# Average pooling 2x2: summing each tile in two halves one behind the other

## Chip, cores, metric

One core of one Trainium2 chip. The metric is device time in microseconds (us); a profiled execution has a span, from the first to the last instruction, about 2 us shorter than its reported time (kernel before: 3100.3 of 3102.09 us).

## Reference

```python
x: float32 (32, 128, 256, 256), kernel_size 2, stride 2
output[:, :, i, j] = np.mean(x[:, :, 2*i:2*i+2, 2*j:2*j+2], axis=(2, 3))    # (32, 128, 128, 128)
```

1073.74 MB are read and 268.44 MB written, with three adds and one multiplication per output.

## The kernel before

A unit is a pair of input rows on each of 128 partitions. A tile has 32 units (8.39 MB in, 2.10 MB out). There are 127 whole tiles and one that is cut into pieces of 16, 8 and 8 units. Two input buffers; SP issues loads, DVE sums, ACT scales and issues stores.

```python
    def sums(it, dst, pieces=1):                       # DVE
        dve.tensor_add(out=it[:, :, 0:w], in0=it[:, :, 0:w], in1=it[:, :, w:]).then_inc(halfway)   # row sum
        take(dve, halfway)
        for g in halves(pieces):                       # column sums
            dve.tensor_add(out=dst[:, g], in0=it[:, g, 0:w:2], in1=it[:, g, 1:w:2]).then_inc(summed)

    def tile_sums(b):
        take(dve, stored[b], 16)
        take(dve, loaded[b], 16)
        sums(ins[b], res[b], 2)

    def tile_scale(b, done, frees=True):               # ACT
        for k, g in enumerate(halves()):
            take(act, summed)
            if k and frees:
                act.sem_inc(free[b])                   # both halves summed: the input buffer is free
            scale(res[b][:, g], done)
    # ... scale_store: tile_scale, wait for both scalings, issue the store
    # ... SP: two loads, then for each further tile take(sp, free[b]); load
```

## Time and profile before

| what | value | how to read it |
|---|---|---|
| time | 3102.11 us | median of three, 0.11 us between lowest and highest |
| DVE, ACT busy | 54%, 16% | neither is near full |
| DMA | 433 GB/s | flat in the steady stretch |
| DVE per tile | 13.33 us from first start to last end, then 10.84 idle | idle until the next load has landed |

The lines behind the last three rows are in the prediction. The starts of the first four tiles, from DVE's timeline (columns: start, duration, engine, line, operation, shapes; in brackets the idle time before and what ended it):

```profile
23.07 8.69 DVE L95 TENSOR_TENSOR in_tile<-in_tile 128x8192 f32<-128x8192 f32 x1 [23.07 <-DVEq L68]
...
42.41 8.69 DVE L95 TENSOR_TENSOR in_tile<-in_tile 128x8192 f32<-128x8192 f32 x1 [6.00 <-DVEq L68]
...
67.11 8.69 DVE L95 TENSOR_TENSOR in_tile<-in_tile 128x8192 f32<-128x8192 f32 x1 [11.37 <-DVEq L68]
...
91.31 8.69 DVE L95 TENSOR_TENSOR in_tile<-in_tile 128x8192 f32<-128x8192 f32 x1 [10.87 <-DVEq L68]
```

Tile starts are landings of loads, since DVE waits for each. It also waits for the store of two tiles earlier (`stored[b]`). From the third on the tile starts are 24.2 us apart. The last store of the kernel:

```profile
3094.17 0.34 ACTq L169 DMA_DIRECT2D out_dram<-res  x1
```

### The profile page before, as it was taken

The numbers are of one execution on the slowest core, as the hardware profiler recorded it, in microseconds if no ns is written. First come the engines' busy times: TensorE is split into PE (matmuls) and PEld (weight loads), VectorE is DVE, ScalarE is ACT, GpSimd is POOL, SyncE is SP. The second block draws the span as 40 slices with busy tenths as digits, with TensorE's granted clock in tenths as the row PEclk, the third lists the DMA queues.
The fourth block names the chain that finished last, engine by engine and source line by source line (L and its number), as shares of the span: only waits on it lengthen the run. The fifth ranks groups of instructions, "written<-read, shape, count | busy, mean of one in ns | idle before, by whom it ended". The sixth has DMA issues, their size and how long they took to land. (4 is left out here: it accounts for less than half of the span.)

```text
span 3100.3 us, 2993 instructions
## 1 busy us (share of the span) xinstructions
DVE 1688.1 (54%) x387; ACT 490.3 (16%) x258; POOL 0.2 (0%) x4
## 2 busy tenths in 40 slices
DVE  4555555555555555555555555555555555555556
ACT  1111111111111111111111111111111111111111
POOL 0000000000000000000000000000000000000000
DMA  9999999999999999999999999999999999999999
GB/s 418 438 438 424 440 431 431 440 426 436 440 426 437 440 423 439 438 424 440 428 435 440 426 436 440 426 437 440 423 440 438 424 440 427 435 440 426 436 440 413
DMA packets 37440, 1342.19 MB, mean 433 GB/s; under 512 B 4160, under 2 KB 4160, under 8 KB 4416
## 3 DMA queue, kind: packets, MB, share of 16 engines
q1 hardware_dynamic: 19008, 1077.94, 80.3%
q10 hardware_dynamic: 18432, 264.25, 19.9%
HBM read 1073.74 MB, written 268.44 MB: 433 GB/s over the span
## 5 line engine op out<-in xcount | busy, mean ns | idle before, releaser
L95 DVE TENSOR_TENSOR in_tile<-in_tile 128x8192 f32<-128x8192 f32 (+1 forms) x130 | 1112.9, 8561 | 1385.7 <-DVEq L68 1385.7
L106 ACT ACTIVATE res<-res 128x2048 f32<-128x2048 f32 (+1 forms) x257 | 489.0, 1903 | 2569.5 <-ACTq L68 2569.5
L98 DVE TENSOR_TENSOR res<-in_tile 128x2048 f32<-128x2048 f32 (+1 forms) x257 | 575.4, 2280 | 19.0
L106 ACT ACT_TABLE_LOAD x1 | 1.3, 1283 | 34.3 <-ACTq L68 34.3
L250 POOL MEMSET const-bfloat16-1.0<- 128x1 bf16 x1 | 0.1, 101 | 0.0
L250 POOL MEMSET const-uint8-127<- 128x1 uint8 x1 | 0.1, 101 | 0.0
L250 POOL MEMSET const-float32-0.0<- 128x1 f32 x1 | 0.1, 98 | 0.2 <-issue 0.2
L250 POOL MEMSET const-float32-1.0<- 128x1 f32 x1 | 0.1, 98 | 0.0
## 6 DMA issues: line engine op xcount, KB each, us to landing
out_dram<-res ACTq DMA_DIRECT2D x125, 2048.0 KB, 32.5
in_tile<-in_x_dram SPq DMA_DIRECT2D x1, 4096.0 KB, 19.9
in_tile<-in_x_dram SPq DMA_DIRECT2D x2, 2048.0 KB, 26.6
out_dram<-res SPq DMA_DIRECT2D x2, 2048.0 KB, 23.7
in_tile<-in_x_dram SPq DMA_DIRECT2D x127, 34.3
out_dram<-res ACTq DMA_DIRECT2D x1, 1024.0 KB, 9.0
out_dram<-res ACTq DMA_DIRECT2D x2, 512.0 KB, 6.3
```

The lines of the kernel that those rows point to most:

```text
L95: dve.tensor_add(out=it[:, :, 0:w], in0=it[:, :, 0:w], in1=it[:, :, w:]).then_inc(halfway)
L98: dve.tensor_add(out=dst[:, g], in0=it[:, g, 0:w:2], in1=it[:, g, 1:w:2]).then_inc(summed)
L106: act.mul(out=dst, in_=dst, mul=0.25).then_inc(done)
L250: nc = _bacc.Bacc("TRN2", target_bir_lowering=False, num_devices=1)
```

## The change

Intent: the first half can be scaled while the second is still summed, because its column sum no longer waits for the row sum of the whole tile.

```diff
-    def sums(it, dst, pieces=1):
+    def sums(it, dst):
         dve.tensor_add(out=it[:, :, 0:w], in0=it[:, :, 0:w], in1=it[:, :, w:]).then_inc(halfway)
         take(dve, halfway)
-        for g in halves(pieces):
-            dve.tensor_add(out=dst[:, g], in0=it[:, g, 0:w:2], in1=it[:, g, 1:w:2]).then_inc(summed)
+        dve.tensor_add(out=dst, in0=it[:, :, 0:w:2], in1=it[:, :, 1:w:2]).then_inc(summed)
 
     def tile_sums(b):
         take(dve, stored[b], 16)
         take(dve, loaded[b], 16)
-        sums(ins[b], res[b], 2)
+        for g in halves:
+            sums(ins[b][:, g], res[b][:, g])
```

(`halves` becomes a plain list of the same two slices.)

More of the change, by code (lines that the diff above doesn't have):

```diff
@@ L82, in _pool_2x2 @@
         a = b
-    def halves(pieces=2):
-        if pieces == 1:
-            return [slice(None)]
-        return [slice(0, TILE // 2), slice(TILE // 2, TILE)]
+    halves = [slice(0, TILE // 2), slice(TILE // 2, TILE)]
     def load(t, b):
         sp.dma_start(out=ins[b], in_=xt[t]).then_inc(loaded[b], 16)
-    def sums(it, dst, pieces=1):
+    def sums(it, dst):
         dve.tensor_add(out=it[:, :, 0:w], in0=it[:, :, 0:w], in1=it[:, :, w:]).then_inc(halfway)
         take(dve, halfway)
-        for g in halves(pieces):
-            dve.tensor_add(out=dst[:, g], in0=it[:, g, 0:w:2], in1=it[:, g, 1:w:2]).then_inc(summed)
+        dve.tensor_add(out=dst, in0=it[:, :, 0:w:2], in1=it[:, :, 1:w:2]).then_inc(summed)
     def tile_sums(b):
@@ L108, in tile_scale @@
     def tile_scale(b, done, frees=True):
-        for k, g in enumerate(halves()):
+        for k, g in enumerate(halves):
             take(act, summed)
```

## The prediction

> **What bounds the kernel now.** I read the page first, then the DMA view of a long steady stretch, then the timeline of one tile and of the end, because a share over the whole run cannot say which wait ends last.
>
> ```profile
> span 3100.3 us, 2993 instructions
> DVE 1688.1 (54%) x387; ACT 490.3 (16%) x258; POOL 0.2 (0%) x4
> DMA  9999999999999999999999999999999999999999
> HBM read 1073.74 MB, written 268.44 MB: 433 GB/s over the span
> ```
>
> No compute engine is near full: DVE, which does all the adds, works 54% of the time. The sixteen DMA engines are busy in every slice. The bytes are fixed by the task: 1342.19 MB at 433 GB/s are 3100 us, the whole span. In a steady stretch of 20 tiles (1400 to 1884 us) the DMA view gives the same 433 in each of its 40 slices, with no dip, so transfers never wait for compute there. One tile is 8.39 MB in and 2.10 MB out; 10.49 MB at 433 GB/s are 24.2 us, and tiles do follow each other at 24.2 us in the timeline (1493.88, 1518.05, 1542.25).
>
> The timeline of one tile:
>
> ```profile
> 1493.88 8.69 DVE L95 TENSOR_TENSOR in_tile<-in_tile 128x8192 f32<-128x8192 f32 x1 [10.87 <-DVEq L68]
> 1502.71 4.50 DVE L98 TENSOR_TENSOR res<-in_tile 128x2048 f32<-128x2048 f32 x2
> 1505.13 1.91 ACT L106 ACTIVATE res<-res 128x2048 f32<-128x2048 f32 x1 [20.02 <-ACTq L68]
> 1507.40 1.91 ACT L106 ACTIVATE res<-res 128x2048 f32<-128x2048 f32 x1 [0.36 <-ACTq L68]
> 1507.56 0.33 SPq L92 DMA_DIRECT2D in_tile<-in_x_dram  x1
> 1509.54 0.34 ACTq L118 DMA_DIRECT2D out_dram<-res  x1
> 1518.05 8.69 DVE L95 TENSOR_TENSOR in_tile<-in_tile 128x8192 f32<-128x8192 f32 x1 [10.84 <-DVEq L68]
> ```
>
> DVE takes 1507.21 - 1493.88 = 13.33 us per tile and then idles 10.84 us until the next load has landed. The load into the buffer just emptied is issued at 1507.56. At that moment the load of the other buffer is still under way, until about 1518.0. So the load queue is refilled 10.5 us before it would run dry. That slack is the number to hold the change against.
>
> At the end the picture is different:
>
> ```profile
> 3065.64 8.69 DVE L95 TENSOR_TENSOR in_tile<-in_tile 128x8192 f32<-128x8192 f32 x1 [10.84 <-DVEq L68]
> 3074.48 4.49 DVE L98 TENSOR_TENSOR res<-in_tile 128x2048 f32<-128x2048 f32 x2
> 3078.89 4.42 DVE L95 TENSOR_TENSOR in_tile<-in_tile 128x4096 f32<-128x4096 f32 x1
> 3083.45 2.29 DVE L98 TENSOR_TENSOR res<-in_tile 128x2048 f32<-128x2048 f32 x1
> 3085.66 2.29 DVE L95 TENSOR_TENSOR in_tile<-in_tile 128x2048 f32<-128x2048 f32 x1
> ...
> 3091.67 1.23 DVE L98 TENSOR_TENSOR res<-in_tile 128x1024 f32<-128x1024 f32 x1
> ```
>
> From the landing of the last whole tile (3065.64) DVE works with no idle time to 3092.90: the three pieces of the remaining tile are there before DVE comes to them (no idle time is listed in front of them). Then come the last scaling (3093.02) and the last store (issued at 3094.17, landed 5.2 us later). So in the last 35 us DVE is on the path, once. But the DMA engines are full there as well: by the view of stretches they still move 381 to 463 GB/s in every 2 us from 3086 to 3098, and stop only after that.
>
> [...]
>
> [...]
>
> [...] the second load ran beside DVE's first adds, from 23.07 to 42.41 us, at 434 GB/s; the first, with DVE idle, at 427, its start-up included. So another order of DVE's reads and writes should not change the transfer rate.
>
> **The change part by part.** For 127 whole tiles DVE's order becomes row sum A, column sum A, row sum B, column sum B, where it was one row sum of both halves and then two column sums. The listing of both instruction streams shows nothing moved on ACT, SP or POOL, only the same instructions at other line numbers. The remaining tile's three pieces are as before.
>
> 1. DVE, removed: 127 row sums of 8192 elements at 8.692 us = 1103.9 us. Added: 254 of 4096 elements at 4.418 us = 1122.2 us. DVE's busy time rises by 18.3 us, from 1688 to about 1706 us (55%). Column sums stay 2.288 us.
> 2. Waits on DVE: a column sum starts 0.14 us after its row sum ends (1502.57 to 1502.71), since it waits for it; with two such pairs there is one more wait of 0.14 us per tile. Where nothing is waited for, the next instruction starts 0.08 us before the end of the one ahead (3078.97 against 3078.89), and that stays one overlap per tile, now between column sum A and row sum B. A half takes 4.418 + 0.14 + 2.288 = 6.85 us; two less the overlap are 13.61 us. The other way: 2 x 4.418 - 8.692 = 0.144, plus 0.14 = 0.28 us per tile more than 13.33.
> 3. ACT: the first scaling starts about 6.98 us into the tile in place of 11.25, so 4.3 us sooner. It buys nothing. The second scaling waits for column sum B, which comes 0.28 us later, and the store waits for both scalings. ACT's idle time before the second scaling grows from 0.36 to about 4.9 us.
> 4. Next load: it is freed by the second column sum, as before, so 0.28 us later. Of 10.5 us of slack, 10.2 stay. In the steady stretch this costs nothing. The fill has less room: the third load is issued at about 36.7 us and the second lands at 42.4, so 5.7 us, still twenty times the delay.
> 5. Store: issued 0.28 us later. It takes 32.5 us to land although 2.10 MB by themselves are 4.8 us at 433 GB/s, so it spends most of that in the queue and a later entry need not be a later landing. Even if the landing moved by 0.28 us, the 10.8 us of DVE's idle time would take it up.
> 6. End: the last whole tile's 0.28 us cannot be absorbed by idle time on DVE, since there is none from there to the end. The last store is issued at about 3094.45. If it then takes the same 5.2 us the end moves by 0.28 us; if it waits behind stores that are still moving, part of that vanishes. I take 0.2.
>
> Sum: 3102.11 + 0 (fill) + 0 (steady) + 0.2 (end) = 3102.3 us.
>
> **The rivals.** (a) The extra 0.28 us adds up tile by tile: 127 x 0.28 = 36 us, 3138 us, 1.2% slower. It would need DVE or the freeing of a buffer to be on the path in every tile. Against it: 10.8 us of idle DVE per tile and a flat 433 GB/s. (b) The pipelining pays: the first half is ready 4.3 us sooner, and if that shortened each tile the gain could be 127 x 4.3 = 546 us. Against it: neither the load nor the store waits for the first half alone, and the bytes at 433 GB/s set 3100 us whatever DVE does. It could only show at the end, and there the last whole tile's second half comes later, not sooner. (c) The small shift changes how packets of loads and stores take turns in the DMA engines. In favour: store landing times depend on the load traffic around them. Against it: [...] the queues stay filled. I allow 2 us either way, mostly at the end, where small stores overlap. (d) The extra DVE traffic slows transfers: the same elements are read and written, and loads show no loss beside DVE; 0 us.
>
> **Range and chances.** Runs of the kernel before lie within 0.11 us of each other. The range is the end's 0 to 0.3 us plus rival (c) and a little for another occasion: 3100.8 to 3104.5. Faster by 2% would need 3040 us, hence 441 GB/s, above the rate seen; slower by 2% would need 62 us, over twice rival (a). So 0.985 for the same, 0.005 faster, 0.01 slower.
>
> **What would show it.** Right: DVE busy near 1706 us; 254 row sums at about 4.42 us; 13.6 us of DVE per tile and about 10.55 us idle after it; ACT waiting about 4.9 us before its second scaling; load issued about 13.96 us after the tile's start in place of 13.68; 433 GB/s in a steady stretch; the last store issued some 28.8 us after the last whole tile's start in place of 28.53. Wrong: any dip in the steady rate, DVE idle time under 10 us per tile, tiles further apart than 24.2 us, or a pause between the last tile's DVE instructions.

(The times of the row sums in steps 1 and 2 are measured in the kernel before: 8.692 us on average for the 127 whole ones, 4.418 us for the one of half the size, in the remaining tile; hence the 2 x 4.418 - 8.692 = 0.144 us that halving costs. 433 GB/s is the rate measured; that it is a limit was not shown.)

## The result and the profile after

| | before | after |
|---|---|---|
| median us | 3102.12 (6 runs, 3102.09 to 3103.85) | 3104.01 (6 runs, 3103.90 to 3104.26) |
| ratio | | 1.0005, 95% interval 0.9992 to 1.0018: same |
| DVE busy us | 1688.1 | 1708.2 |

Ratios are the mean time of one kernel's runs over that of the other's runs of the same rounds, so not quite the ratio of the medians quoted. The verdict is "same", as forecast, but 1.9 us were added where 0.2 were expected, and the runs of each kernel mostly lie too close together for that to be noise. The experiments go after those 1.9 us.

The page of the changed kernel:

```profile
span 3102.4 us, 3247 instructions
DVE 1708.2 (55%) x514; ACT 490.3 (16%) x258; POOL 0.2 (0%) x4
```

One steady tile of the changed kernel, from its timeline:

```profile
1496.04 4.42 DVE L91 TENSOR_TENSOR in_tile<-in_tile 128x4096 f32<-128x4096 f32 x1 [10.55 <-DVEq L68]
1500.61 2.29 DVE L93 TENSOR_TENSOR res<-in_tile 128x2048 f32<-128x2048 f32 x1
1502.82 4.42 DVE L91 TENSOR_TENSOR in_tile<-in_tile 128x4096 f32<-128x4096 f32 x1
1503.02 1.91 ACT L102 ACTIVATE res<-res 128x2048 f32<-128x2048 f32 x1 [15.44 <-ACTq L68]
1507.38 2.29 DVE L93 TENSOR_TENSOR res<-in_tile 128x2048 f32<-128x2048 f32 x1
1509.86 1.91 ACT L102 ACTIVATE res<-res 128x2048 f32<-128x2048 f32 x1 [4.93 <-ACTq L68]
1510.03 0.33 SPq L88 DMA_DIRECT2D in_tile<-in_x_dram  x1
1512.01 0.34 ACTq L114 DMA_DIRECT2D out_dram<-res  x1
1520.21 4.43 DVE L91 TENSOR_TENSOR in_tile<-in_tile 128x4096 f32<-128x4096 f32 x1 [10.53 <-DVEq L68]
```

This is the predicted tile: 13.63 us of DVE (1509.67 - 1496.04), 10.53 us idle, ACT waiting 4.93 us before its second scaling, the load issued at 1510.03, 13.99 us after the tile's start, and the next tile 24.17 us later. Per tile, nothing was lost. The steady 20 tiles from 1400 to 1884 us moved 433 GB/s in all 40 slices, as before.

The time is already missing at the third tile. The starts of tiles two to four of the changed kernel, from the same view:

```profile
42.58 4.42 DVE L91 TENSOR_TENSOR in_tile<-in_tile 128x4096 f32<-128x4096 f32 x1 [5.71 <-DVEq L68]
...
69.34 4.42 DVE L91 TENSOR_TENSOR in_tile<-in_tile 128x4096 f32<-128x4096 f32 x1 [13.12 <-DVEq L68]
...
93.53 4.42 DVE L91 TENSOR_TENSOR in_tile<-in_tile 128x4096 f32<-128x4096 f32 x1 [10.55 <-DVEq L68]
```

The third tile starts at 69.34 against 67.11, 2.23 us late (the second only 0.17), and the last whole tile at 3067.80 against 3065.64, 2.16 us late. The end adds nothing:

```profile
3096.64 0.34 ACTq L165 DMA_DIRECT2D out_dram<-res  x1
```

The last store is issued 28.84 us after the last whole tile's start (before: 28.53), the predicted 0.3 us more; but from that start to the end of the span it is 34.60 us (3102.4 - 3067.8) against 34.66; in a second profile of the changed kernel (e0 below) it is 34.78.

**Where 2.2 us go in a queue that never runs dry.** The trace has a record of every DMA packet (start, duration, size, queue; a load packet is one partition's 64 KiB, a store packet 16 KiB), but not its engine. I gave each packet to the engine whose packet before it had just ended. This yields 16 chains with 8 load packets each per load (in the three profiles below without exception; in others a few packets are misplaced). In the steady stretch a load packet takes 2418 ns and a store packet 611, and they alternate while a store is in progress. End of the last whole tile's load, us after the first data packet:

```
                          median of 16 engines   slowest engine   its lag
kernel before                    3061.98             3062.28        0.30
changed kernel, 1st profile      3062.41             3064.45        2.04
changed kernel, 2nd profile      3062.04             3064.17        2.13
```

A check that needs no assignment: the sixteen completion marks of each load. The slowest mark of the last whole tile's load lies behind the median mark by the same 0.30, 2.04 and 2.13 us.

So fifteen engines are nearly as early as before; one is 2 us behind, and DVE starts after the last of the sixteen marks: at 3065.64 for 3064.86 us of the span in the kernel before, at 3067.80 for 3067.04 in the first profile of the changed kernel. In the first profile that engine had five slow load packets in a row between 42 and 59 us of the span (3160, 2774, 2698, 2781, 2926 ns for a usual 2418, so 2.25 us over); on the other engines no load packet of that time is more than 0.5 us over. After that every engine works without pause at the same pace, and the lag stays 2.04 us from tile 4 to tile 126: the late engine does not catch up.

### The profile page after: what moved, and what is told of

Same layout as the page of the kernel before. It is cut to its first block, busy times and chain, and to the rows that moved or that the text cites. A ratio compares the mean times of both kernels' runs of the same rounds, so it can differ in the third digit from the quotient of the medians.

```text
span 3102.4 us, 3247 instructions
## 1 busy us (share of the span) xinstructions
DVE 1708.2 (55%) x514; ACT 490.3 (16%) x258; POOL 0.2 (0%) x4
## 5 line engine op out<-in xcount | busy, mean ns | idle before, releaser
L91 DVE TENSOR_TENSOR in_tile<-in_tile 128x4096 f32<-128x4096 f32 (+1 forms) x257 | 1132.0, 4405 | 1349.5 <-DVEq L68 1349.5
L93 DVE TENSOR_TENSOR res<-in_tile 128x2048 f32<-128x2048 f32 (+1 forms) x257 | 586.9, 2284 | 37.7
## 6 DMA issues: line engine op xcount, KB each, us to landing
out_dram<-res ACTq DMA_DIRECT2D x125, 2048.0 KB, 32.1
```

Of the source, the lines that this page charges most:

```text
L93: dve.tensor_add(out=dst, in0=it[:, :, 0:w:2], in1=it[:, :, 1:w:2]).then_inc(summed)
```

## The experiments

All against the kernel before on the same chip. First: is the loss tied to the first tiles?

**e0, the changed kernel again.**

> The changed kernel once more, unaltered, on this chip and beside more runs of the kernel before. Fill theory (about 2.2 us are lost before the third tile, because one DMA engine falls behind there): 3104.0 us, the third tile starting near 69.3 us. Chance theory (two states that either kernel can fall into, as the one run of the kernel before at 3103.85 us hints): some runs near 3102.4 and some near 3104, in both kernels.

Measured 3104.22 us (3103.76 to 3104.34). The time repeats: 11 runs of the changed kernel, all between 3103.76 and 3104.34. The place does not. Here the third tile came at 67.23 us, on time, and the lag grew later. Start of a tile less 24.18 us times its number (a lag that stays shows as a constant):

```
tile                     2      30      60      90     126
kernel before          18.75   18.85   18.87   18.92   18.96
changed, 1st profile   20.98   21.01   21.05   21.08   21.12
changed, 2nd (e0)      18.87   18.95   19.97   20.44   20.98
```

So my fill theory falls as a rule: the lag can arise at the start or creep in over hundreds of microseconds, to about the same 2 us.

**e1, control: the kernel before, its first two tiles taken out of the loop.**

```diff
-        with dve.Fori(0, whole // 2):
+        tile_sums(0, False)          # False: as in the kernel before
+        tile_sums(1, False)
+        with dve.Fori(1, whole // 2):
```

(The calls in the loop and after it get `False` too.)

> The kernel before's order of sums for every tile, with the first two tiles taken out of DVE's loop: the control for the next two. Every theory expects 3102.1 us and a third tile near 67.1 us; if it comes near 3104, the place of DVE's instructions alone decides and the fill theory in its simple form falls.

Measured 3103.16 us (3102.52 to 3104.02). Its profiled run, 3102.62, has the tiles on time (last one at 3065.81 us) and a span of 3100.5; 2.1 us lie outside the span, where the kernel before has 1.8. That 0.3 us does not come from the order of the sums (it also shows in e3, k2 and k8; I do not know its origin). It does not explain all: two runs have spans of 3100.4 and 3100.5 us, as in the kernel before, but three have 3101.0, 3101.0 and 3101.9. So the control missed its expectation: code that keeps the order of the sums and the moments of issue was slower in three of five runs. These have no trace.

**e2, only the first tile half by half.** (Edit: as e1, with `tile_sums(0, True)`.)

> Only the first tile is summed half by half; the other 126 as in the kernel before. Fill theory: nearly the whole loss comes back, 3103.7 to 3104.0 us, third tile near 69.3 us. Rival, a cost of every tile or of the last one: 3102.1 us.

Measured 3102.42 us, but in two groups: 3102.13, 3102.18, 3102.42 and 3103.59, 3103.71. The profile is of a late one: its third tile came at 67.55, and the drift set in after tile 66, in tiles summed in the old order. Neither expectation holds.

**e3, the first two tiles whole, all others half by half.**

> The first two tiles as in the kernel before, the other 125 half by half. Fill theory: only the end's 0.28 us are left, 3102.4 us, third tile near 67.1 us. Rival, a cost of every tile or of the last one: 3104.0 us.

Measured 3104.55 us (3104.35 to 3105.17), all five late. In its profile the third tile came at 69.10 us, before a single half-by-half tile had been summed. So the early kick is not an effect of the first tiles' order; but a kernel whose steady tiles go half by half was late in all its runs.

That left the steady tile. The change does two things there: the first scaling comes 4.3 us sooner, and load and store are issued 0.3 us later. Two kernels separate them.

**k1, the kernel before with a small add on DVE, which delays both issues by 0.27 us.**

```diff
+            if k:   # between the two column sums of a tile
+                dve.tensor_add(out=pad[:, 0:195], in0=it[:, 0, 0:195], in1=it[:, 1, 0:195]).then_inc(padded)
             dve.tensor_add(out=dst[:, g], in0=it[:, g, 0:w:2], in1=it[:, g, 1:w:2]).then_inc(summed)
```

(Cut: a wait for `padded` after the loop.)

> The kernel before with a small extra add of 195 elements between a tile's two column sums, so that the second one, and with it the next load's issue and the store's, come about 0.28 us later, as in the changed kernel; the order of the sums stays. Phase theory (the 0.3 us later issue of load and store, in each tile, decides whether one DMA engine falls about 2 us behind the others): most runs at 3103.5 to 3104.3 us. Rival, the earlier first scaling on ACT does it: most runs at 3102.1 to 3102.4. Rival, chance: a mixture.

Measured 3104.09 us (3103.96 to 3104.17), all five. The timeline of one of its tiles:

```profile
1494.54 8.69 DVE L97 TENSOR_TENSOR in_tile<-in_tile 128x8192 f32<-128x8192 f32 x1 [10.63 <-DVEq L70]
1503.38 2.29 DVE L102 TENSOR_TENSOR res<-in_tile 128x2048 f32<-128x2048 f32 x1
1505.59 0.35 DVE L101 TENSOR_TENSOR pad<-in_tile 128x195 f32<-128x195 f32 x1
...
1508.49 0.33 SPq L94 DMA_DIRECT2D in_tile<-in_x_dram  x1
1510.47 0.34 ACTq L124 DMA_DIRECT2D out_dram<-res  x1
```

The order is the old one, the load is issued 13.95 us after the start (before: 13.68; changed kernel: 13.99), and the time is the changed kernel's.

**k2, the changed kernel with the first scaling held back.**

```diff
-        for g in halves:
-            sums(ins[b][:, g], res[b][:, g])
+        it, dst = ins[b], res[b]
+        for k, g in enumerate(halves):
+            dve.tensor_add(out=it[:, g, 0:w], in0=it[:, g, 0:w], in1=it[:, g, w:]).then_inc(halfway)
+            take(dve, halfway)
+            if k:
+                take(dve, first)
+                dve.sem_inc(summed)
+            dve.tensor_add(out=dst[:, g], in0=it[:, g, 0:w:2], in1=it[:, g, 1:w:2]).then_inc(summed if k else first)
```

> The changed kernel, but the first half's scaling is let go only when the second row sum is done, about 11.4 us into a tile as in the kernel before; load and store are issued when the changed kernel issues them. Phase theory: 3104.0 us as in the changed kernel. Rival, the earlier scaling does it: 3102.1 to 3102.4 us.

Measured 3105.10 us (3104.74 to 3105.25). The first scaling began 11.58 us after the tile's start, as late as in the kernel before (11.25), and the loss stayed. The extra waits moved the load's issue to 14.19 us. With k1 this shows that the loss does not need ACT's earlier work: the later issue is enough. Load and store moved together in both kernels (and in all that follow), so which of the two issues matters was not tested.

What the drift consists of is seen in k1. From 200 to 3000 us its late engine's 926 store packets took 0.99 us longer in all than 611 ns each, and its 925 load packets 0.46 us longer than 2418 ns each. These 1.45 us are nearly the whole growth of its lag (0.54 to 2.07 us). About half of them lie around the issue of the next load (13.95 us after a tile's start): 44 of the store packets that begin at 13.6 us took 12 ns more on average, and 33 of the load packets that begin at 14.2 us took 7 ns more. The rest lies elsewhere, for instance in 18 of the store packets that begin at 22.7 us, where no transfer is issued. In the kernel before, the same count over all sixteen engines comes to 0.10 us; in k7 and k9 (below) it is zero.

**k8, the changed kernel, issue another 0.30 us later.** (Edit: k1's small add, 215 elements, ahead of the second column sum.)

> The changed kernel with a small add of 215 elements ahead of the second column sum of each tile, so that load and store are issued another 0.30 us later: the load about 14.3 us after a tile's start, past the moment (14.2 us) at which the last DMA engine goes from a store's packet to a load's; in the changed kernel the issue (13.99 to 14.32) covers that moment. Phase theory: the drift stops, most runs at 3102.1 to 3102.7 us though DVE does more. Rival, any later issue harms: 3104.0 us or more.

Measured 3105.09 us (3104.80 to 3105.28); load issued at 14.28 us; the drift again begins after tile 48. My guess of the harmful moment was wrong: it does not end at 14.2 us.

**k9, the kernel before, issue 1.0 us later.** (Edit: k1's small add with 886 elements.)

> The kernel before with 1.0 us more on DVE ahead of the second column sum: the load is issued about 14.7 us after a tile's start, in the middle of a load's packet, the store at 16.7 inside a store's packet. Phase theory: no drift, most runs at 3102.1 to 3103.2 us (up to 1 us for the end). Rival, the later the issue the worse: 3104 us or more, as with the 0.28 us.

Measured 3101.91 us; four runs at 3101.87 to 3102.01, one at 3104.26. With the load issued at 14.67 us the lag of the slowest engine stays 0.23 us to the end. So "later is worse" falls: among the moments tried it is a window. k9 also has k1's extra instruction and semaphore, so these are not what makes k1 late. The table gives the load's issue after the tile's start, the runs (late: some 2 us above the kernel before), and the lag of the slowest engine at the last whole tile in the profiled run, by the completion marks:

```
                                                                                        lag, us
13.68 us  kernel before          29 of 33 runs at 3101.95 to 3102.49, 4 at 3103.41 to 3103.99   0.30
13.68     e1, e2                 5 of 10 at 3102.13 to 3102.62, 5 at 3103.16 to 3104.02         0.33, 1.45
13.95     k1                     5 of 5 late                                                    2.07
13.99     changed kernel, e3     16 of 16 late                                                  2.04, 2.13, 1.98
14.19     k2                     5 of 5 late                                                    2.25
14.28     k8                     5 of 5 late                                                    2.30
14.67     k9                     4 of 5 on time                                                 0.23
18.55     k7 (below)             4 of 4 on time                                                 0.21
```

(e2's profiled run is one of its late ones.) The moment of issue is not all: e1 and e2 issue as the kernel before does and were late more often.

The end of k9's timeline also settles what a later last store costs:

```profile
3065.46 8.69 DVE L97 TENSOR_TENSOR in_tile<-in_tile 128x8192 f32<-128x8192 f32 x1 [9.84 <-DVEq L70]
...
3094.99 0.34 ACTq L175 DMA_DIRECT2D out_dram<-res  x1
```

The store is issued 29.53 us after the last whole tile's start, 1.0 us later than in the kernel before, yet the span (3100.1 us) ends 34.64 us after that start, as there (34.66). So here a last store issued 1.0 us later did not move the end.

**The slack itself.** Four kernels load DVE with more adds per tile, written over later:

```diff
+        for _ in range(extra):
+            dve.tensor_add(out=res[b], in0=ins[b][:, :, 0:w_out], in1=ins[b][:, :, w:w + w_out]).then_inc(halfway)
+            take(dve, halfway)
         for g in halves:
```

**k4, two more in tiles 0 to 125.**

> The changed kernel with two adds of 4096 elements more in each of the first 126 tiles, whose results are written over: 2 x (4.42 + 0.14) = 9.1 us of DVE per tile more, 22.7 us in all, still under the 24.18 us of a tile's transfers and inside the slack of 10.2 us. If the steady stretch is bound by transfers as predicted: 3102 to 3106 us. If DVE's time counts tile by tile: 126 x 9.1 = 1150 us more.

**k5, three more.**

> Three such adds more, 13.7 us per tile: DVE then needs 27.3 us per tile, more than the transfers' 24.18, and the slack is overdrawn. Expected: tiles 27.4 us apart, 3102 + 126 x 3.2 = 3505 us, DVE busy nearly throughout and DMA below 433 GB/s. If it stayed near 3104, the slack would be larger than read.

k4 took 3455.6 us and my expectation fell, though DVE's 22.7 us per tile are less than 24.18. k5 took 3614 us (two runs; expected 3505); 512 us more over 126 tiles are 28.2 us per tile. In k4, tiles came in pairs: two back to back, then 10 us of idle DVE. From 1495 to 1525 us DVE worked 29.3 of 30 us, from 1525 to 1536.5 us 1.5 of 11.5. My reading, an estimate: the other load had landed, with no new one queued, while DVE was still at work (transfers begun from 1495 to 1505 us come to 288 GB/s, from 1505 to 1515 to 457). For the last 3 of these 10 us the load was there and DVE waited for a store. The suspect was the fill: in k4 no packet begins from 40 to 46 us, while DVE works 5.85 of these 6 us, and in the kernel before the second load lands only 19.3 us after the first (23.07 to 42.41), where later loads are 24.2 us apart.

**k7, one more add, from the third tile on.**

> The changed kernel with one add of 4096 elements more (4.56 us) in tiles 2 to 125, none in the first two. Transfers bind the steady stretch: 3102 to 3104.5 us, 24.18 us between tiles, about 6 us of idle DVE per tile. If each tile's DVE time counted: 124 x 4.56 = 565 us more.

**k6, the same add in the first two tiles too.**

> The same add in all of the first 126 tiles, the first two too. The third load is then issued about 41.8 us after the start, when the second has just finished at about 41.4 us: the queue runs dry for some 2 us. If the loss in the two kernels with more adds came from the fill, this one loses about 2 to 3 us more than the one with the add from the third tile on, or falls into the same uneven rhythm of two tiles and a pause. If the fill has nothing to do with it, both take the same time.

k7: 3102.47 us (3102.36 to 3102.54); 4.56 us more DVE per tile cost 0.35 us over the whole run (3102.12 for the kernel before in the same rounds), and this was 1.5 us faster than the changed kernel that it is built from. k6: 3268.07 us (3263.11 to 3271.84). The two differ only in the first two tiles. From k6's timeline, the first tile's last column sum, the issue of the third load and the start of the second tile:

```profile
38.82 2.29 DVE L93 TENSOR_TENSOR res<-in_tile 128x2048 f32<-128x2048 f32 x1
...
41.50 49.27 SPq L88 DMA_DIRECT2D in_tile<-in_x_dram  x3
42.22 4.42 DVE L99 TENSOR_TENSOR res<-in_tile 128x4096 f32<-128x4096 f32 x1 [1.11 <-DVEq L68]
...
71.89 4.42 DVE L99 TENSOR_TENSOR res<-in_tile 128x4096 f32<-128x4096 f32 x1 [11.45 <-DVEq L68]
```

(The SPq line merges three issues; its start is the third load's.) By the packet records the sixteen engines end the second load between 41.30 and 41.73 us, and the third load, issued at 41.50, begins between 42.48 and 43.14: the engines stood idle for about 1 us. The third tile starts 29.7 us after the second. What it waited for last is not the load, which landed at 68.27 us, but the first tile's store, which landed at 71.30. It was issued at 43.33, after the third load had begun, and no longer ends together with that load; in the kernel before it was issued at 39.42, 2 us before the third load began (41.35 to 41.93), and both ended at 66.35. From then on the tiles alternate, one after 11 us of idle DVE and the next after 3.6, and in each of them the store lands last, 3.03 us behind the load (one load and one store packet) or 0.61 (one store packet), the last tile apart. The even rhythm never comes back. The rate in a steady stretch (1400 to 1884 us) falls from 433 to 412 GB/s: of these 484 us each engine is idle for 8 on average and loses 16 more to load packets that take longer (2522 ns on average for 2418).

No version beat the kernel before by more than the 0.2 us of k9, so none is offered as an improvement.

## Why the prediction was right or wrong

- **What bounds the kernel: right.** Transfers at 433 GB/s; k7 adds 124 x 4.56 = 565 us of DVE time, and its median is 0.35 us above that of the kernel before.
- **Steps 1 to 3 (DVE, waits, ACT): right.** DVE busy 1708.2 for 1706 predicted (the column sums averaged 2.292 us, not 2.288, and the row sums 4.421); 13.63 us per tile for 13.61; ACT's wait 4.93 us for 4.9.
- **Step 4, the steady stretch: right; the fill: mis-sized.** The load came at 13.99 us for 13.96 and cost nothing through the slack. But "5.7 us, still twenty times the delay" counted from the issue to the landing as DVE sees it (42.4 us). The first engine is done with the second load at 41.35 us, the third load is issued at 36.80, and a load issued when the engines were idle (k6) moved its first data about 1 us later. So some 3.6 us are left, an estimate from these figures. One add of 4.56 us there was already too much (k6). For 0.28 us it made no difference.
- **Step 5, the store: right in the outcome, wrong in its safety margin.** Its median landing was 32.1 us after issue for 32.5, so the 0.28 us later issue was absorbed in the queue. But DVE's 10.8 us of idle time could not have taken up a later landing: that idle time ends with the store's landing as much as with the load's (within 0.01 us of each other), and in k6, where the store lands later, DVE waits for it.
- **Step 6, the end, 0.2 us: wrong.** The last store was issued 0.3 us later and the end came at nearly the same distance from the last whole tile's start (34.60 us, 34.78 in the second profile, 34.66 before); k9 shows that even 1.0 us is hidden.
- **Rival (c): it was the outcome.** "I allow 2 us either way, mostly at the end" had the size, but not the place or the sign. That the range held is therefore partly luck: the 2 us were an allowance and not worked out. What happened instead: the landing of each load slips by about 2 us against the sixteen engines' common pace, because one engine falls behind, at the start or gradually. The argument against it, that the queues stay filled, is the step that failed: in the filled queue one engine's lag of 2.04 us stayed to the end. Its 2 us were left out of the sum; that is the term that was missing.
- **Rivals (a), (b), (d): did not occur.** Tiles stay 24.17 us apart, nothing was gained by the earlier scaling (the changed kernel took no less time), and the steady rate is the same. Two slips in the working: 62 us are 1.7 times rival (a)'s 36, not over twice; and the range's lower end leaves 1.3 us below 3102.11, not the 2 us allowed.

What is shown: the extra 1.9 us is one DMA engine's lag of about 2 us, and moving both issues so that the load's comes 13.95 to 14.28 us after a tile's start (four moments tried) is enough for it, in every run of five kernels, whatever the order of the sums. What stays open: whether the load's issue or the store's does it; why packets take longer, around the issue and elsewhere; where the window's edges are; what slows one engine in the first 60 us in some runs (two of the profiles); why the lag stops near 2 us; and why kernels outside the window fall into it now and then, e1 and e2 in half of their runs.

## What to carry to other kernels

In this kernel, whose DMA queue never ran dry, a compute engine's later finish cost next to nothing (1.9 us of 3102), and the 0.3 us that splitting the instruction added to each tile was hidden. Look for the slack in the fill as well: in k6 a queue that ran dry once, for about 1 us, was followed by an uneven rhythm to the end and a run 5% longer (3268.07 us for 3102.12). Count that slack to the end of the transfers, not to the landing that an engine waits for, and look up every transfer that an engine waits for, the stores too (in k6 the store landed 3.03 us after the load). Here a difference of less than 0.1% between two kernels came with nothing but the moment at which the next transfers were issued (k1, load at 13.95 us for 13.68 after a tile's start: 3104.09 us for 3102.24 in the same rounds; k9, with the same kind of extra add and the load at 14.67 us, took 3101.91); try the same delay in the old kernel before crediting such a difference to the change.
